# Projections ahead of attention: q with k and p0 with p1 as seven-product pairs in a decoder layer on one Trainium2 core

## The chip, the core and the metric

The kernel runs on one core of a Trainium2 chip. Its engines are TensorE (PE, matrix products, with a queue of its own for loading weights, PEld), VectorE (DVE), ScalarE (ACT) and GpSimd (POOL); SyncE (SP) mostly issues transfers (DMA). Each works through its own queue in order and they meet through semaphores. The metric is the device time of one execution in microseconds (us). A time quoted as the median comes from three executions; a profile shows one execution.

## The reference, cut to what matters

One layer of a hybrid decoder, 512 tokens by 1024 channels, float32. The part that the change touches is the input projection and the attention behind it:

```python
proj = h @ w_in[l]                      # 512x1024 by 1024x4096
q, k, v, p, g = jnp.split(proj, [...])  # 512, 512, 512, 512, 2048 columns
y_attn = moba_attention(q, k, v, rel_bias) @ w_branch_attn[l]     # 8 heads of 64
y_pool = multiscale_pool(p, w_pool_group[l], pool_scale[l]) @ w_branch_pool[l]
gates = sigmoid(g).reshape(B, S, 2, D)
mixed = gates[:, :, 0] * y_attn + gates[:, :, 1] * y_pool
h = layer_norm(ALPHA * h + mixed @ w_out[l], ...)
a, u = split(h @ w_ffn_in[l], 2)        # gated feed-forward with a causal convolution
h = layer_norm(ALPHA * h + (gelu(conv(a)) * u) @ w_ffn_out[l], ...)
```

With 512 tokens the block selection of the attention takes every past block, so it is causal attention with a relative bias. The pooling branch takes, for each of four groups of 128 channels, the mean over the last 2, 4, 8 or 16 tokens minus the token, and multiplies it by a 128x128 matrix.

## The kernel before, in words

**Numbers.** Every float32 operand of a large product is split in a high part (a rounded copy, made by ACT, line 69) and a low part (the difference, made by DVE, line 70), and a product is the sum of three matmuls: high by high, high by low, low by high (`mm3`, lines 211, 214, 215). PE does nothing but such matmuls, the transposes and the small products of attention.

**Tiles.** The projections are computed transposed: a *tile* is 128 output channels by 512 tokens, eight chunks of 128 input channels deep, so 24 matmuls of 512 columns (`in_tile`). Its weights are one *chunk*, 128 by 1024 numbers, loaded by SP into `wraw`, split into `whi` and `wlo`, which are rings of five; chunks are asked for in the order of a list, three ahead of the use (`LEAD`, `weights`, `fetch`). There are four tiles each of q, k and p, and sixteen of g, the gate logits. v is computed first, for all four blocks of tokens at once.

**Seven-product pairs.** Where two tiles are computed together, the product of a 2x2 block matrix is done with seven block products in place of eight (`seven`): products with the chunks A, X, D and Y of the weights, two quarters each for A, X and Y, one for D, each against a quarter of x or a sum of quarters of x. A product is 12 matmuls of 256 columns. A is a plain tile of weights, D is a half of the other one. X is made by a copy (SP) and an accumulating transfer on top of it (POOL, line 163). Y is made of A and X by two sums on DVE (line 173). The sums of quarters of x are called nT1, T3, nT2 and T4 and are formed on DVE (lines 232 and 235, `t_form`) and split. The partial results are copied out by ACT and summed by DVE (lines 252 to 266); the last product of a pair, its closing, is issued behind the first two of the next pair (`flush`). In the kernel before this form is used for eight of the gate tiles (four pairs, `sag`, `sbg`, `scg` in the trace) and for the feed-forward's input (`saf`, `sbf`, `scf`), not for q, k and p.

**The order of the work.** v, q0, k0, p0; then, for each pair of heads, the scores of two heads, two transposes and the product with v, with one tile behind each of the four steps (`bg`, which also issues the pooling product `zb` of a p tile two tiles later). The tiles in this place are the rest of q, k and p and seven g tiles; one g tile remains behind the last product with v. Then come the branch products (`br`), the gate pairs, and the rest of the layer.

**Attention, a head.** `scores`: eight matmuls of high-precision q by k (q in one tile of high and low halves, k in two tiles `k1` and `kl`, made from the tile in `q_done`, `k_done`: lines 382 to 394); DVE adds the bias strip and takes the maximum (line 458); ACT takes the exponentials and sums (line 464); DVE the reciprocal; POOL scales the rows (line 469). `trans`: ten transposes on PE (line 483) and copies out. `pv`: the product with v for two heads (line 496).

**Pooling.** `pool_in`: ACT copies the tile (402), POOL makes the windowed sums by up to four additions (407), DVE makes the difference (410 to 412), which is split. `pool_out` is the small product, `zb`.

Of the kernel before, what the change touches and what calls it, by code (L numbers as in the profile page):

```python
# [19 lines left out]
H = 8  # L20
# [13 lines left out]
TMP = 4  # L34
WARM = 7
NKEEP = 12
# [9 lines left out]
def layer_kernel(ctx: ExitStack, tc: tile.TileContext, xT, x, w_v, w_c, rel_bias, invcnt, w_group,  # L46
# [18 lines left out]
    def split(hi, lo, src, copy=None):  # L65
        if copy:
            copy(hi, src)
        else:
            nc.scalar.activation(hi, src, AF.Copy)  # L69
        nc.vector.tensor_tensor(lo, src, hi.bitcast(F32), op=ALU.subtract)  # L70
# [10 lines left out]
    C0 = len(chunks)  # L81
    chunks += [w_c[first[n] + j] for n, j in order]
# [11 lines left out]

    for f in range(KT - 1):
        add(("br", f), w_br[f])
# [53 lines left out]
    homes = {("g", "A"): araw, ("f", "A"): araw}  # L150
# [133 lines left out]
    keep = keepp.enter_context(tc.tile_pool(name="keep", bufs=1))  # L284
    attn = ExitStack()
    aw = attn.enter_context(tc.tile_pool(name="aw", bufs=2))
# [11 lines left out]
    def load_x(kt, xr, c=slice(0, S), copy=None):  # L298
        state["x"] = nc.sync.dma_start(xr[:, c], xT[kt * P:(kt + 1) * P, c])
        split(xT_hi[:, kt, c], xT_lo[:, kt, c], xr[:, c], copy)  # L300

    for kt in range(KT):
        xr = aw.tile([P, S], F32, tag="tmp", name=f"xr{kt}", bufs=TMP)
        if kt == 0:
            load_x(kt, xr, slice(0, 256), nc.vector.tensor_copy)
            fetch(early=lambda: load_x(kt, xr, slice(256, 512), nc.vector.tensor_copy))
        else:
            load_x(kt, xr)
            if kt % 2 == 0:
                fetch()  # L310
# [15 lines left out]
    wg_raw = aw.tile([P, 4, P], F32, tag="strip", name="wg_raw", bufs=3)  # L326
    nc.sync.dma_start(wg_raw, w_group)
    wg_hi = aw.tile([P, 4, P], F32R, name="wg_hi", bufs=1)
    wg_lo = aw.tile([P, 4, P], F32R, name="wg_lo", bufs=1)
# [4 lines left out]
    F_sb = aw.tile([H, STRIP], F32, tag="pp", name="F_sb", bufs=3)  # L334
# [8 lines left out]
    strips = {}  # L343

    def load_strip(h):
        strips[h] = aw.tile([P, S], F32, tag="strip", name=f"strip{h}", bufs=3)
# [6 lines left out]
    vv = aw.tile([P, NT, H * DH], F32, name="vv", bufs=1)  # L353
# [15 lines left out]
    gates = keep.tile([P, NKEEP, S], F32, name="gates")  # L369
    zT = keep.tile([P, 4, S], F32, name="zT")  # L370
    oT = keep.tile([P, 4, S], F32, name="oT")
# [6 lines left out]
    def q_done(p, b):  # L378
        for e in range(2):
            own, oth = slice(e * DH, (e + 1) * DH), slice((1 - e) * DH, (2 - e) * DH)  # L380
            t = aw.tile([P, S], F32R, tag="q1", name=f"q1_{2 * p + e}", bufs=3)
# [4 lines left out]

    def k_done(p, b):
        for e in range(2):
            own, oth = slice(e * DH, (e + 1) * DH), slice((1 - e) * DH, (2 - e) * DH)
            hi = aw.tile([P, S], F32R, tag="k1", name=f"k1_{2 * p + e}", bufs=3)  # L390
            lo = aw.tile([P, S], F32R, tag="kl", name=f"kl_{2 * p + e}", bufs=3)
            for half in (own, oth):
                nc.scalar.activation(hi[half, :], b[own, :], AF.Copy)
                nc.vector.tensor_tensor(lo[half, :], b[own, :], hi[own, :].bitcast(F32), op=ALU.subtract)
# [3 lines left out]
    def pool_in(j, b):  # L398
        w = POOL_WINDOWS[j]
        pt = aw.tile([P, PAD + S], F32, tag="tmp", name=f"pt{j}", bufs=TMP)  # L400
        nc.gpsimd.memset(pt[:, :PAD], 0.0)
        nc.scalar.activation(pt[:, PAD:], b, AF.Copy)
        cur, sh = pt, 1
        while sh < w:
            nxt = aw.tile([P, PAD + S], F32, tag="tmp", name=f"pw{j}_{sh}", bufs=TMP)
# [3 lines left out]
        d = aw.tile([P, S], F32, tag="tmp", name=f"dif{j}", bufs=TMP)  # L409
# [3 lines left out]
        dh = aw.tile([P, S], F32R, tag="difh", name=f"difh{j}", bufs=2)  # L413
# [611 lines left out]
```

## Time and profile before

| | us |
|---|---|
| median of 3 executions | 645.15 (643.87 to 646.44) |
| the profiled execution | 644.98 |
| its span, first to last instruction | 643.3 |
| PE busy in it | 631.4 (98%) |
| DVE busy | 472.4 (73%) |
| ACT busy | 346.4 (54%) |
| POOL busy | 119.8 (19%) |

The mean granted clock of PE is 0.995 of full speed.

A row of a group reads: line of the kernel, engine, operation, output <- inputs, count, then busy time, mean duration in ns, and the idle time of the engine ahead of these instructions with what ended it. A row of waits: what waited <- what it waited for, then us in total, times, the longest. A row of the timeline: start, duration, engine, line, operation, output <- inputs, count. A row of the table by windows: the window in us, its length, then busy us (and instructions) of PE, PEld, DVE, ACT and POOL, the granted clock of PE, the share of the DMA engines' time, and GB/s. A row of transfers: output <- input, queue, count, size, median us from issue to landing. In the timeline several instructions of a kind stand in one row, with x and their count. A matmul's own duration overlaps the next one's: what a matmul costs in a full stream is the distance of two starts.

### The profile page before, as it was taken

The page shows a single profiled execution, that of the slowest core. Times are in us where ns is not written, and L with a number is a line of the kernel's source. Part 1 is how long each engine was busy: PE and PEld are TensorE (multiplying, and loading weights), DVE is VectorE, ACT ScalarE, POOL GpSimd, SP SyncE. Part 2 cuts the span into 40 slices and gives each one's busy share as a digit, 9 for nine tenths or more (in the row PEclk, how much of TensorE's full clock was granted, in tenths as well). Part 3 has the DMA queues.
Part 4 walks back from the last instruction along what each step waited for, and adds up shares of the span by engine and source line. Part 5 has one row for each costly group of instructions (what it writes and reads, how often), then busy time and mean ns, then how long its engine had stood idle before and what let it go on. Part 6 is the DMA issues. An engine that isn't in the chain of part 4 may idle for free.

```text
span 643.3 us, 9708 instructions
## 1 busy us (share of the span) xinstructions
PE 631.4 (98%) x3730; PEld 555.0 (86%) x3730; DVE 472.4 (73%) x698; ACT 346.4 (54%) x505; POOL 119.8 (19%) x161
## 2 busy tenths in 40 slices
PE   9999999999999999999999999999999999999994
PEld 6888787878788998889999999999998888888884
DVE  6456665564884787499776889888889649788596
ACT  6547556675624557225544566556666346556352
POOL 1505260213052111110010101011002002123202
PEclk9999999999999999999999999999999999999998
DMA  8733222115366415714086576776638956899905
GB/s 303 261 123 103 83 82 83 67 66 186 110 185 158 115 41 191 275 52 165 1 236 171 147 202 160 211 167 198 148 100 297 273 149 131 208 187 206 250 2 130
DMA packets 35294, 100.06 MB, mean 156 GB/s; under 512 B 3880, under 2 KB 4136, under 8 KB 34992
## 3 DMA queue, kind: packets, MB, share of 16 engines
q1 hardware_dynamic: 23920, 67.96, 31.2%
q0 software_dynamic: 10752, 30.43, 23.4%
q10 hardware_dynamic: 576, 1.05, 0.4%
q8 instruction: 29, 0.48, 0.3%
q14 instruction: 17, 0.14, 0.1%
HBM read 96.26 MB, written 3.17 MB: 155 GB/s over the span
## 4 chain that ended last, share of the span: by engine, by line
PE 89%; DMA 4%; DVE 3%; POOL 2%; ACT 1%; issue 1%; SPq 0%; DVEq 0%; ACTq 0%; POOLq 0%
PE fi L214 5%; PE fi L215 5%; PE fi L211 5%; PE saf L211 4%; PE saf L215 4%; PE saf L214 4%; PE v L367 3%; PE g L211 2%; PE g L215 2%; PE g L214 2%; PE br L214 2%; PE br L215 2%; PE wo L214 2%; PE br L211 2%; PE wo L211 2%; PE wo L215 2%
## 5 line engine op out<-in xcount | busy, mean ns | idle before, releaser
L70 DVE TENSOR_TENSOR wlo<-wraw,whi 128x1024 fp32r<-128x1024 f32 (+1 forms) x69 | 84.4, 1228 | 33.3 <-ACT whi L69 32.9
L69 ACT ACTIVATE whi<-wraw 128x1024 fp32r<-128x1024 f32 (+1 forms) x68 | 70.3, 1038 | 59.9 <-PE g L214 8.6
L214 PE MATMUL fi<-hT_lo,whi 128*128 128x512 f32 (+1 forms) x168 | 56.7, 339 | 0.0
L215 PE MATMUL fi<-hT_hi,wlo 128*128 128x512 f32 (+1 forms) x168 | 56.7, 339 | 0.0
L211 PE MATMUL fi<-hT_hi,whi 128*128 128x512 f32 (+1 forms) x168 | 56.4, 340 | 0.0
L70 DVE TENSOR_TENSOR wlo<-araw,whi 128x1024 fp32r<-128x1024 f32 x36 | 43.7, 1221 | 14.5 <-ACT whi L69 13.8
L69 ACT ACTIVATE whi<-araw 128x1024 fp32r<-128x1024 f32 x36 | 37.9, 1060 | 22.1 <-PE br L214 6.4
L163 POOL DMA_DIRECT2D xraw<-in_w_fi x14 | 16.9, 1210 | 162.3 <-DMA xraw<-in_w_fi 85.5
L69 ACT ACTIVATE whi<-tw 128x1024 fp32r<-128x1024 f32 (+1 forms) x30 | 29.3, 983 | 23.6 <-PE fi L214 10.4
L70 DVE TENSOR_TENSOR wlo<-tw,whi 128x1024 fp32r<-128x1024 f32 (+1 forms) x30 | 33.3, 1126 | 7.9 <-ACT whi L69 7.8
L215 PEld LDWEIGHTS fi<-hT_hi,wlo 128*128 128x128 f32 x168 | 31.9, 190 | 3.4
L214 PEld LDWEIGHTS fi<-hT_lo,whi 128*128 128x128 f32 x168 | 31.9, 190 | 3.4
L211 PEld LDWEIGHTS fi<-hT_hi,whi 128*128 128x128 f32 x168 | 31.6, 190 | 3.4
L214 PE MATMUL saf<-hT_lo,whi 128*128 128x256 f32 x112 | 31.6, 282 | 0.0
L211 PE MATMUL saf<-hT_hi,whi 128*128 128x256 f32 x112 | 31.6, 282 | 0.0
L215 PE MATMUL saf<-hT_hi,wlo 128*128 128x256 f32 x112 | 31.5, 282 | 0.0
L211 PE MATMUL sbf<-T_hi,whi 128*128 128x256 f32 x112 | 31.3, 280 | 0.0
L211 PE MATMUL saf<-nT_hi,whi 128*128 128x256 f32 x112 | 31.3, 279 | 0.0
L215 PE MATMUL saf<-nT_hi,wlo 128*128 128x256 f32 x112 | 31.3, 279 | 0.0
L215 PE MATMUL sbf<-T_hi,wlo 128*128 128x256 f32 x112 | 31.2, 279 | 0.0
L214 PE MATMUL saf<-nT_lo,whi 128*128 128x256 f32 x112 | 31.2, 279 | 0.0
L214 PE MATMUL sbf<-T_lo,whi 128*128 128x256 f32 x112 | 31.2, 279 | 0.0
(301 smaller groups left out, 2006.9 us busy)
## 6 DMA issues: line engine op xcount, KB each, us to landing
wraw<-in_w_c SPq DMA_DIRECT2D x20, 512.0 KB, 3.5
tw<-in_w_fo POOLq DMA_DIRECT2D x20, 512.0 KB, 7.0
wraw<-in_w_fi SPq DMA_DIRECT2D x16, 512.0 KB, 3.9
araw<-in_w_fi SPq DMA_DIRECT2D x14, 512.0 KB, 4.5
xraw<-in_w_fi SPq DMA_DIRECT2D x14, 512.0 KB, 4.3
xraw<-in_w_fi POOLq DMA_DIRECT2D x14, 512.0 KB, 6.0
tw<-in_w_fo SPq DMA_DIRECT2D x10, 512.0 KB, 5.0
wraw<-in_w_fo SPq DMA_DIRECT2D x10, 512.0 KB, 9.0
```

The costliest lines, as they stand in the source:

```text
L69: nc.scalar.activation(hi, src, AF.Copy)
L70: nc.vector.tensor_tensor(lo, src, hi.bitcast(F32), op=ALU.subtract)
L163: nc.gpsimd.dma_start(v, bass.AP(tensor=a.tensor, offset=a.offset, ap=[[pst, pn], [u.offset + S - a.offset, 2], [est, S]]), accum_op=ALU.add)
L211: ins = nc.tensor.matmul(out_, wh, ah, start=start, stop=False, **kw)
L214: nc.tensor.matmul(out_, wh, al, start=False, stop=False, **kw)
L215: nc.tensor.matmul(out_, wl, ah, start=False, stop=stop, **kw)
L367: nc.tensor.matmul(bs[j], xs_[j][a], (wh, wl)[b], start=kt == 0 and n == 0, stop=False)
```

## The change

The projections that attention needs are computed ahead of it. After v come p2 and p3 as plain tiles, then five seven-product pairs: p0 with p1, and q with k four times (q0 with k0 and so on). The four sums of x that these need (named `iT...`, `inT...`) are formed in the raw x tiles at the start, and these tiles then serve as homes of the X and D chunks, A chunks go to the ring `wraw`. The second tile of a pair comes out negated, so `k_done` and the copy in `pool_in` get a factor of -1. For each pair ACT or the closing sums leave q and k raw in buffers (`rq`, `rk`); `heads(p)` makes q and k of two heads from them, for the first pair at once, for the others at every second head of the attention.

In attention, scores run two heads ahead of the transposes, and eight g tiles fill the eight steps, one a head, the last of them behind the last transposes. The split of the pooling output zT is done during heads 4 to 7 in program order. The sigmoids of the gate tiles are held back until the last copy of the attention's output. The memory is laid out anew: a pool for the projection phase (`pw`), one for what both phases use (`av`) and one for attention (`aw`). The core of the diff:

```diff
-    order = [("q", 0), ("k", 0), ("p", 0), ("p", 1)]
-    spare = [("p", 2), ("p", 3)] + [("g", 8 * g + f) for f in range(GSEVEN) for g in range(2)]
-    for p in range(1, pairs):
-        order += [("q", p), ("k", p), spare.pop(0), spare.pop(0)]
-    order += spare
...
+    for j in PLAIN:
+        add(("p", j), w_c[first["p"] + j])
+    add_seven(("i", 0), w_c[first["p"]], w_c[first["p"] + 1])
+    for p in range(pairs):
+        add_seven(("i", 1 + p), w_c[first["q"] + p], w_c[first["k"] + p])
+    fill = [("g", 8 * g + f) for f in range(GSEVEN) for g in range(2)]
+    for n, j in fill:
+        add((n, j), w_c[first[n] + j])
...
-    homes = {("g", "A"): araw, ("f", "A"): araw}
+    homes = {(n, "A"): araw for n in "igf"}
...
+    xr = [pw.tile([P, 4, S], F32, name=f"xr{n}") for n in range(2)]
...
+    def heads(p):
+        q_done(p, raw_q[p])
+        k_done(p, raw_k[p])
...
+    with tc.issue_after(state["xlo"].ins):
+        t_form(parts[0], ti, xr[0][:, :, t1], xr[0][:, :, t2], xr[1][:, :, t1], xr[1][:, :, t2])
+    for n in parts[1:]:
+        t_form(n, ti, xr[0][:, :, t1], xr[0][:, :, t2], xr[1][:, :, t1], xr[1][:, :, t2])
+    homes["i", "X"] = lambda n: xr[0][:, n % 2 * 2:n % 2 * 2 + 2, :].rearrange("p a c -> p (a c)")
+    homes["i", "D"] = lambda n: xr[1][:, n % 2, :]
+    for j in PLAIN:
+        in_tile("p", j)
...
+    def pool_done(ba, u):
+        pool_in(0, ba)
+        pool_in(1, u, -1.0)
+
+    def heads_done(p, ba):
+        raw_q[p] = av.tile([P, S], F32, tag="rq", name=f"rq{p}")
+        nc.scalar.activation(raw_q[p], ba, AF.Copy)
+        if p == 0:
+            heads(0)
+
+    for n in range(1 + pairs):
+        if n == 0:
+            u, done = xr[1][:, 3, :], pool_done
+        else:
+            u = raw_k[n - 1] = av.tile([P, S], F32, tag="rk", name=f"rk{n - 1}")
+            done = lambda ba, u, p=n - 1: heads_done(p, ba)
+        seven(("i", n), (xT_hi, xT_lo), ti, xr[1][:, 2, n % 2 * 256:n % 2 * 256 + 256], u, done)
+        if n == 2:
+            for j in PLAIN:
+                pool_out(j)
+        elif n == 4:
+            pool_out(0)
+            pool_out(1)
+    flush()
...
-    bg(3)
-    for p in range(pairs):
-        scores(2 * p)
-        bg()
-        scores(2 * p + 1)
-        bg()
-        trans(2 * p)
-        bg()
-        trans(2 * p + 1)
-        bg()
-        pv(p)
-    bg(len(todo))
+    scores(0)
...
+    scores(1)
+    for h in range(H):
+        if h % 2 == 0 and h + 2 < H:
+            heads(h // 2 + 1)
+        if h < H - 1:
+            in_tile(*fill.pop(0))
+        if h + 2 < H:
+            scores(h + 2)
+        trans(h)
+        if h >= 4:
+            split(zT_hi[:, h - 4, :], zT_lo[:, h - 4, :], zT[:, h - 4, :])
+        if h == H - 1:
+            in_tile(*fill.pop(0))
+        if h % 2:
+            pv(h // 2)
...
-            for g in range(2):
-                nc.scalar.activation(gslot[8 * g + f], gslot[8 * g + f], AF.Sigmoid)
+            with tc.issue_after(state["o"].ins):
+                for g in range(2):
+                    nc.scalar.activation(gslot[8 * g + f], gslot[8 * g + f], AF.Sigmoid)
```

The order in which each engine finally issues its instructions is set by a scheduler from this program order, and is known before the kernel runs; "the built order" below means that.

More of the change, by code (lines that the diff above doesn't have):

```diff
@@ L34 @@
 TMP = 4
+PLAIN = (2, 3)
 WARM = 7
-NKEEP = 12
 KH = NF // 2
@@ L325, in layer_kernel @@
                             compare_op=ALU.is_equal, fill=0.0)
-    wg_raw = aw.tile([P, 4, P], F32, tag="strip", name="wg_raw", bufs=3)
     nc.sync.dma_start(wg_raw, w_group)
-    wg_hi = aw.tile([P, 4, P], F32R, name="wg_hi", bufs=1)
-    wg_lo = aw.tile([P, 4, P], F32R, name="wg_lo", bufs=1)
+    wg_hi, wg_lo = (pw.tile([P, 4, P], F32R, name=f"wg_{q}") for q in ("hi", "lo"))
     split(wg_hi, wg_lo, wg_raw)
@@ L529, in layer_kernel @@
     bp = bra.enter_context(tc.tile_pool(name="bp", bufs=1, reuse_waits="tile"))
-    zT_hi = bp.tile([P, 4, S], F32R, name="zT_hi")
-    zT_lo = bp.tile([P, 4, S], F32R, name="zT_lo")
     oT_hi = bp.tile([P, 4, S], F32R, name="oT_hi")
     oT_lo = bp.tile([P, 4, S], F32R, name="oT_lo")
-    for k in range(4):
-        split(zT_hi[:, k, :], zT_lo[:, k, :], zT[:, k, :])
+    more = bp.tile([P, 4, S], F32, name="more")
     for k in range(4):
@@ L565, in merged @@
         mts[f] = a
-    unused = [gates[:, n, :] for n in range(2 * GSEVEN, NKEEP)]
+    unused = [more[:, n, :] for n in range(4)]
     forms = list(parts)
```

106 lines of the change are left out of this document (50 added, 56 removed).

## The prediction

> **What bounds the kernel now.** I read the busy times first, then what TensorE (PE) waits for, then the table by stretches of time.
>
> ```profile
> PE 631.4 (98%) x3730; PEld 555.0 (86%) x3730; DVE 472.4 (73%) x698; ACT 346.4 (54%) x505; POOL 119.8 (19%) x161
> ```
>
> ```profile
> PE warm_ps L296 <- DVE warm L293: 1.2, 1, 1.2
> PE fod L214 <- DVE wlo L70: 0.6, 1, 0.6
> PE zb L211 <- ACT difh L69: 0.6, 2, 0.3
> PE v L367 <- DVE whi L275: 0.3, 1, 0.3
> ```
>
> ```profile
> 25.00:45.00 20.00, 20.00 (x91) 16.60 (x90) 7.90 (x10) 9.96 (x14) 1.69 (x3) 1.00 0.54 176
> ...
> 345.00:485.00 140.00, 140.00 (x1176) 139.57 (x1175) 118.98 (x165) 83.75 (x124) 14.45 (x12) 1.00 0.65 170
> ```
>
> PE is busy 98% of the span, and the four rows of its waits add up to 2.7 us: matmul time is the time, and any idle time that the change gives PE in the stage it rewrites is added almost whole. In 25 to 45 us (plain projection tiles) VectorE (DVE) works 7.9 of 20 us and could take more. In 345 to 485 us, seven-product pairs of the feed-forward, PE is full but DVE is at 119 of 140 us: this method is paid for by DVE.
>
> **What a pair saves.** In the timeline of PE, q starts at 26.99 and k at 32.43; in the chain of waits the last products of four feed-forward pairs start at:
>
> ```profile
> 26.99 0.39 PE L211 MATMUL q<-xT_hi,whi 128*128 128x512 f32 x1
> 32.43 0.39 PE L211 MATMUL k<-xT_hi,whi 128*128 128x512 f32 x1
> ...
> 50.04 0.28 PE L454 MATMUL sc<-k,q 128*128 128x256 f32 x1
> 51.33 0.40 PE L211 MATMUL q<-xT_hi,whi 128*128 128x512 f32 x1
> ...
> 58.06 0.47 PE L211 MATMUL k<-xT_hi,whi 128*128 128x512 f32 x1
> 58.37 0.39 PE L214 MATMUL k<-xT_lo,whi 128*128 128x512 f32 x1
> ```
>
> ```profile
> 413.79 0.36 PE saf L215 x3
> 473.27 0.36 PE saf L215 x3
> ```
>
> A plain tile of 24 matmuls takes 32.43 - 26.99 = 5.44 us (0.227 each), two take 10.88. Six pairs lie between 413.79 and 473.27: 59.48 / 6 = 9.91 us a pair of 84 matmuls (0.118 each, 1.42 for a product of 12). A pair saves 0.97 us, the five new ones (p0 with p1, four of q with k) **-4.84 us**, as long as PE is fed. The rows also give the eight score matmuls of a head, 51.33 - 50.04 = 1.29 us.
>
> **The order.** More groups of attention now alternate with tiles. 58.06 to 58.37 is 0.31, so a switch costs 0.31 - 0.23 = 0.08 us. The built order has some 12 switches more, because pv is cut by gate tiles: +1.0. The two waits of zb (0.6, above) go, as the pooled inputs are ready long before the pairs at which zb now stands: -0.6. Together **+0.4**.
>
> **Stalls at the first pair.** The chunk X of a pair is a sum of weight quarters: a copy issued by SyncE (SP), an accumulating transfer on top issued by GpSimd (POOL), then the split. Its home is the first half of the raw x, which T3 still uses, so the copy waits until T3 is formed and split on DVE. Rows:
>
> ```profile
> xraw<-in_w_fi SPq DMA_DIRECT2D x14, 512.0 KB, 4.3
> xraw<-in_w_fi POOLq DMA_DIRECT2D x14, 512.0 KB, 6.0
> quad<-in_w_c POOLq DMA_DIRECT2D x4, 512.0 KB, 7.9
> ```
>
> ```profile
> 17.50 0.68 DVE L70 TENSOR_TENSOR xT_lo<-xr,xT_hi 128x512 fp32r<-128x512 f32 x1
> 19.59 0.69 DVE L70 TENSOR_TENSOR wg_lo<-wg_raw,wg_hi 128x512 fp32r<-128x512 f32 x1 [1.41 <-ACT wg_hi L69]
> ...
> 46.61 0.69 DVE L410 SCALAR_TENSOR_TENSOR dif<-pw,pt 128x512 f32<-128x512 f32 x1 [0.23 <-POOL pt L401]
> 47.33 0.29 DVE L458 CUSTOM_DVE_ANT_0 pp<-sc,strip 128x128 f32<-128x128 f32 x1
> 47.55 0.42 DVE L458 CUSTOM_DVE_ANT_0 pp<-sc,strip 128x256 f32<-128x256 f32 x1
> 47.90 0.15 DVE L411 TENSOR_TENSOR dif<-pw,cinv 128x1 f32<-128x1 f32 x1
> 49.05 0.08 DVE L458 DVE_READ_ACCUMULATOR2_ANT nm<- 128x1 f32 x1
> ```
>
> ```profile
> L70 DVE TENSOR_TENSOR wlo<-wraw,whi 128x1024 fp32r<-128x1024 f32 (+1 forms) x69 | 84.4, 1228 | 33.3 <-ACT whi L69 32.9
> ```
>
> ```profile
> L235 DVE SCALAR_TENSOR_TENSOR quad<-quad,quad x2: 1212/1213/1214, 175.4 to 180.5; 128x1024 f32<-128x1024 f32 x2
> ...
> L173 DVE TENSOR_TENSOR araw<-xraw,araw x14: 679/687/694, 339.3 to 470.4; 128x512 f32<-128x512 f32 x14
> ```
>
> (a) The last split of x ends at 17.50 + 0.68 = 18.2. Behind it DVE has, in the built order, three forms (1.21), the low parts of two weight tiles and two forms (1.23) and wg_lo (0.69): 9.2 us, so 27.4. The copy lands 4.3 later, at 31.7; the accumulate 6.0 to 7.9 after that (the two POOL rows), 37.7 to 39.6; two Y sums (0.69) and wlo7 (1.23) follow, 40.3 to 42.2. PE wants it at 4.71 (start of v, as before) + 22.28 (v) + 10.88 (p2, p3) + 2.83 (two products) = 40.7. Between -0.4 and 1.5 I take **+0.9**, nearer the 7.9 row, which is the one that reads this weight tensor. (b) The next splits, wlo9 and wlo10, come 1.76 us apart (1.23, and half of dif2's 0.69 + 2 x 0.15 between them) against a product of 1.42: 2 x 0.33 = **+0.66** (bounds 0 and 1.2). (c) The T4 product waits for a high part that is queued on ScalarE (ACT) behind that of the next X chunk, and so for its accumulate: 0 to 1.2, **+0.6**.
>
> (d) POOL takes its queue in order. The accumulate of the third X chunk stands ahead of p3's four pool additions, and waits for a copy that starts when wlo7 is done (T). Rows:
>
> ```profile
> L407 POOL TENSOR_TENSOR pw<-pt 128x527 f32<-128x527 f32 x4 | 4.7, 1165 | 28.6 <-ACT pt L402 28.5
> ...
> L163 POOL DMA_DIRECT2D xraw<-in_w_fi x14 | 16.9, 1210 | 162.3 <-DMA xraw<-in_w_fi 85.5 <-DVE fT L264 27.4 <-DVE wlo L70 16.8
> ```
>
> T + 4.3 + 1.2 (issue) + 4 x 1.17 = T + 10.2. Then DVE does dif3 (0.69, twice 0.15), two sums (0.42 each), wlo12 (0.68) and the last sum of pair 0 (0.42), all queued at or behind dif3: T + 13.1. PE needs that sum for the closing product of pair 0 after 84 matmuls, T + 9.9 + the 1.3 of (b) and (c) = T + 11.2. **+1.9**, bounds 0 (POOL reaches the additions earlier) and 4.9 (below).
>
> The rest of the pairs: DVE has some 38 us of work in 41.5 us of products between wlo7 and the last pair's chunk (my count of the built order by these durations), ACT 31, so no more stalls there.
>
> **Stalls at the hand-over to attention.** Rows of the timeline for one head, and of the groups:
>
> ```profile
> L394 DVE TENSOR_TENSOR kl<-k,k 64x512 fp32r<-64x512 f32 x16 | 11.0, 687 | 6.8 <-ACT k L393 6.7
> ```
>
> ```profile
> 51.19 0.40 ACT L464 ACTIVATE pp<-pp,nm 128x128 f32<-128x128 f32 x1
> 53.29 0.19 ACT L464 ACTIVATION_READ_ACCUMULATOR pp<-pp,nm 128x1 f32 x1
> ```
>
> ```profile
> 53.80 3.04 POOL L469 TENSOR_SCALAR pp<-pp,rs 128x128 f32<-128x128 f32 x4 [0.51 <-DVE nm L461]
> ...
> 141.45 2.07 POOL L469 TENSOR_SCALAR pp<-pp,rs 128x128 f32<-128x128 f32 x4 [18.35 <-PE g L215]
> ```
>
> Call E the end of head 1's scores. The closing product of the last pair waits for a DVE sum that is queued behind wlo29 and the two kl of head 4. wlo29's high part waits for a ring slot that PE frees only 0.6 before E, and head 4's k waits for E itself. DVE: wlo29 to E + 1.7, kl twice 0.69 to 3.1, the sum 0.42: E + 3.5. PE is idle until then. Then DVE goes on with q1_4 (0.69), the score reductions of heads 0 and 1 (47.33 to 49.13 in the rows above is 1.8 with two dif operations in it, so 1.7 each), three zT_lo (0.69 at 0.64 pitch), the negated maximum (0.2): E + 9.9. Exponentials 51.19 to 53.48, say 2.1 in a row without the load: 12.0. Reciprocal 0.2, and the first three of four scalings on POOL (6 of 10 columns of 2.07 to 3.04: 1.2 to 1.8): E + 13.7. The first transposes need these. PE's own work from E is 1.42 + 5.44 + 1.29 = 8.15. PE loses 13.7 - 8.15 = **+5.5** (3.5 ahead of the closing product, 2.0 ahead of the transposes). Bounds: 3 (wlo29 and the zT_lo slip in elsewhere) and 7. From there PE has 8.9 us a head against DVE 6.9 and ACT 6.6; I find no other stall. The last move is the load of quads, whose place is now used by attention: it starts after the last pv.
>
> ```profile
> 163.57 0.50 PE L211 MATMUL g<-xT_hi,whi 128*128 128x512 f32 x1
> ...
> 207.22 0.28 PE L211 MATMUL sag<-xT_hi,whi 128*128 128x256 f32 x1
> ```
>
> In the kernel before, the last pv ends at 163.57 and the gate pairs that use quads start at 207.22; without the tile between, 38.2 us remain, and load, four forms, copy and accumulate are needed within them: some 28 us by the durations above and my count of DVE's order (the load taken as an accumulate's 6.0 to 7.9). Cost nothing; if DVE's branch work delays the forms by over 10 us, the excess is added.
>
> **Sum.** -4.84 + 0.4 + 0.9 + 0.66 + 0.6 + 1.9 + 5.5 = +5.1. Against the profiled execution, 644.98 us, that is 650.1; the median of the runs, 645.15, lies 0.17 above it, so 650.3. A change of 0.5% is 3.2 us, about what a measurement of this kernel tells from no change.
>
> [...]
>
> ```profile
> 635.00:640.00 5.00, 0.00 (x0) 0.00 (x0) 3.85 (x10) 0.80 (x2) 0.72 (x1) 0.71 0.78 208
> 640.00:643.30 3.30, 0.00 (x0) 0.00 (x0) 0.00 (x0) 0.00 (x0) 0.00 (x0) 0.50 0.32 122
> ```
>
> PE's last matmul ends near 634, and the granted clock is 0.71 over the next 5 us and 0.50 after: it falls to half some 3 us into idleness. So the gap may cost a stretch at half clock; what it costs is hidden as long as PE waits 2.0 us for the transposes anyway, so I add nothing. [...]
>
> **Rivals.** (1) Faster: the stalls are hidden, because the scheduler's order leaves DVE more room than my hand chain gives: the five pairs keep their 4.84 less 0.4, and 645.15 - 4.4 = 640.7. For it: DVE is idle 12 of 20 us in 25 to 45. Against it: the sum for E + 3.5 is in DVE's order behind work that is released by E. It decides if all stalls together stay under 1.2 us (4.4 less the 3.2 of 0.5%). (2) No change: the pair phase runs without stalls, and only the hand-over costs: -4.84 + 0.4 + 5.5 gives 646.2. For it: (a) to (d) rest on landing times that may be 2 us shorter. (3) Slower than forecast: the additions and accumulates on POOL slow down beside DVE. One row has it:
>
> ```profile
> 83.88 1.92 POOL L407 TENSOR_TENSOR pw<-pw 128x525 f32<-128x525 f32 x1
> ```
>
> At 1.92 for each of p3's four additions (d) grows by 4 x 0.75 = 3.0, the three of p0 and p1 by 2.3, and each accumulate at 7.9 in a pair phase where DVE is 92% full turns its delay into PE's: 655 to 658. [...]
>
> **How the numbers follow.** Forecast 0.45 (648.4 to 653.5), rival 1 0.12, rival 2 0.25 (643 to 648), rival 3 0.18. The range 643.5 to 657 leaves out rival 1 and the top of rival 3, about 0.18. Faster 0.12, same 0.25, slower 0.63.
>
> **What would show it.** PE's waits in the profile after: a row for the first X product of pair 0 near 41 us, one for its closing product on a DVE sum, one of about 3.5 for the last pair's closing product, one of about 2 for tr on POOL's scaling. Pairs free of waits should start 9.9 us apart. If q and k pairs run at 9.9 and tr doesn't wait, rival 1 holds. Wrong I would be above all if DVE's pitch is shorter than its busy time, or if accumulates land in 4 us.

## The result, and the profile after

The changed kernel takes 661.29 us (median, 660.70 to 662.12), the kernel before 644.65 (643.87 to 646.44) in the same comparison: a ratio of 1.0255 (1.0229 to 1.0281). It is slower by 16.6 us, where +5.1 was forecast, and lies above the forecast range. The profiled execution of the changed kernel took 662.12, its span is 660.4 and its mean granted clock 0.987. From here *before* and *after* are the two kernels.

The busy times of after, and what PE waits for:

```profile
PE 638.0 (97%) x3910; PEld 566.3 (86%) x3910; DVE 497.9 (75%) x741; ACT 355.0 (54%) x530; POOL 133.0 (20%) x166
```

```profile
PE sai L212 <- DVE sai L266: 6.1, 2, 4.1
PE sbi L212 <- ACT whi L69: 3.7, 1, 3.7
PE sai L216 <- DVE wlo L70: 1.3, 1, 1.3
PE warm_ps L306 <- DVE warm L303: 1.2, 1, 1.2
PE sbi L216 <- DVE wlo L70: 0.9, 1, 0.9
```

Waits of 2.7 us have become 13.2. The waits for zb are gone, as forecast. PE's busy time has also risen, by 6.6 us, although five pairs should need 4.84 us less: waits alone don't tell the story.

Where the time went is told by the first branch product, which both kernels reach after the same work. In the timelines of before and of after:

```profile
169.14 0.39 PE L211 MATMUL br<-zT_hi,whi 128*128 128x512 f32 x1
```

```profile
187.24 0.50 PE L212 MATMUL br<-zT_hi,whi 128*128 128x512 f32 x1
```

After is 18.1 us late there, and wins 1.0 behind it (span 17.1 longer). So everything happened in the stage that was rewritten, and what follows is unhurt. In this stage, PE has three long gaps. They are shown here (timeline of after; the bracket is the idle time ahead of the instruction), and below them the table by windows for the time behind each gap:

```profile
44.13 0.39 PE L212 MATMUL sbi<-iT_hi,whi 128*128 128x256 f32 x1 [3.73 <-ACT whi L69]
...
59.34 0.58 PE L212 MATMUL sai<-xT_hi,whi 128*128 128x256 f32 x1 [2.03 <-DVE sai L266]
...
107.86 0.58 PE L212 MATMUL sai<-xT_hi,whi 128*128 128x256 f32 x1 [4.06 <-DVE sai L266]
```

```profile
45.90:49.10 3.20, 3.20 (x17) 3.20 (x17) 3.20 (x6) 2.29 (x4) 0.00 (x0) 0.50 0.67 208
59.30:62.30 3.00, 2.96 (x14) 2.96 (x15) 2.97 (x4) 1.69 (x4) 0.13 (x2) 0.50 0.90 186
63.00:91.00 28.00, 26.65 (x216) 25.87 (x215) 26.03 (x39) 20.81 (x35) 5.29 (x5) 1.00 0.40 108
107.50:113.50 6.00, 5.64 (x19) 5.04 (x20) 5.99 (x21) 3.58 (x5) 1.18 (x2) 0.50 0.39 125
```

The first is the first X product of pair 0, the second its closing product, the third the closing product of the last pair. After each, the granted clock (third number from the end) is 0.50 for 3 to 6 us. What half clock does to a matmul is seen in two pairs of neighbours:

```profile
111.01 0.63 PE L215 MATMUL g<-xT_lo,whi 128*128 128x512 f32 x1
111.44 0.63 PE L216 MATMUL g<-xT_hi,wlo 128*128 128x512 f32 x1
...
114.21 0.40 PE L212 MATMUL g<-xT_hi,whi 128*128 128x512 f32 x1
114.44 0.40 PE L215 MATMUL g<-xT_lo,whi 128*128 128x512 f32 x1
```

A pitch of 0.43 us in place of 0.23, so 47% of such a stretch is lost: 1.5 + 1.4 + 2.8 = 5.7 us in the three. In the row of 63 to 91 us, DVE works 26.0 of 28.0 us: the pairs leave it little room.

The last part is the product with v. One of before and its counterparts in after (timeline; x counts the matmuls that ran without another in between):

```profile
71.90 2.37 PE L496 MATMUL ob<-PT,vv 128*64 128x512 f32 x16
```

```profile
128.02 1.07 PE L543 MATMUL ob<-PT,vv 128*64 128x512 f32 x2
129.02 0.51 PE L212 MATMUL g<-xT_hi,whi 128*128 128x512 f32 x1
...
133.60 1.07 PE L543 MATMUL ob<-PT,vv 128*64 128x512 f32 x4
...
136.19 1.51 PE L543 MATMUL ob<-PT,vv 128*64 128x384 f32 x10
137.63 0.39 PE L501 MATMUL sc<-k,q 128*128 128x256 f32 x1
```

Sixteen matmuls in one go take 2.3 us from start to start of the next (71.90 to 74.21). Cut into 2, 4 and 10 they take 1.00 + 1.00 + 1.44 = 3.44. Each is 128*64 in the rows, where the projections are 128*128, and the two heads write different halves of the output. In before the sixteen start in pairs, the first at 71.90 and 71.91 us, the second at 72.38 and 72.39: two heads' matmuls run beside each other. Where the scheduler draws them apart, they no longer do: in the first piece of after the two matmuls of 512 columns, of one head alone, start at 128.02 and 128.50. They take 1.00 us, and at that price the sixteen, which have 320 columns on average, would take some 5 us (an estimate) and not 2.3. Three of the four products with v are cut like this.

### The profile page after: what moved, and what is told of

Read it like the earlier page. It is cut to its first block, busy times and chain, and to the rows that moved or that the text cites. A ratio compares the mean times of both kernels' runs of the same rounds, so it can differ in the third digit from the quotient of the medians.

```text
span 660.4 us, 10178 instructions
## 1 busy us (share of the span) xinstructions
PE 638.0 (97%) x3910; PEld 566.3 (86%) x3910; DVE 497.9 (75%) x741; ACT 355.0 (54%) x530; POOL 133.0 (20%) x166
## 4 chain that ended last, share of the span: by engine, by line
PE 86%; DVE 4%; POOL 4%; DMA 3%; issue 2%; ACT 1%; SPq 0%; DVEq 0%; POOLq 0%
PE fi L212 4%; PE fi L216 4%; PE fi L215 4%; PE saf L212 4%; PE saf L216 4%; PE saf L215 4%; POOL F_sb L347 3%; PE g L212 2%; PE g L216 2%; PE g L215 2%; PE br L212 2%; PE wo L216 2%; PE br L216 2%; PE br L215 2%; PE wo L215 2%; PE wo L212 2%
## 5 line engine op out<-in xcount | busy, mean ns | idle before, releaser
L70 DVE TENSOR_TENSOR wlo<-wraw,whi 128x1024 fp32r<-128x1024 f32 (+1 forms) x59 | 72.2, 1231 | 18.7 <-ACT whi L69 18.6
L69 ACT ACTIVATE whi<-wraw 128x1024 fp32r<-128x1024 f32 (+1 forms) x58 | 59.6, 1034 | 45.6 <-DMA wraw<-in_w_fo 9.0
L70 DVE TENSOR_TENSOR wlo<-araw,whi 128x1024 fp32r<-128x1024 f32 x46 | 57.8, 1263 | 10.1 <-ACT whi L69 9.4
L69 ACT ACTIVATE whi<-araw 128x1024 fp32r<-128x1024 f32 x46 | 48.2, 1058 | 19.7 <-PE saf L215 6.1
L212 PE MATMUL saf<-hT_hi,whi 128*128 128x256 f32 x112 | 31.7, 283 | 0.0
```

The source lines that it names most:

```text
L70: return nc.vector.tensor_tensor(lo, src, hi.bitcast(F32), op=ALU.subtract)
L212: ins = nc.tensor.matmul(out_, wh, ah, start=start, stop=False, **kw)
```

## The experiments

Unless it says otherwise, each kernel computes the same as after. Ratios are to before on the same chip; where after is compared, its 1.0255 is meant, and by the intervals a difference of two ratios is uncertain by some 2 us.

**The first gap: POOL's queue.** The X chunk's accumulate is in POOL's queue, and what stood ahead of it is in the timeline of after:

```profile
14.46 17.46 POOL L347 COPY F_sb<-rel 8x1 f32<-8x1 f32 x32 [12.91 <-DMA rel<-in_rel_bias]
32.23 0.76 POOL L349 DMA_DIRECT2D F_d<-F_sb  x1 [0.32 <-POOL F_sb L347]
34.78 1.69 POOL L353 DMA_DIRECT2D strip<-F_d  x3 [1.79 <-DMA F_d<-F_sb]
36.45 2.55 POOL L164 DMA_DIRECT2D xr<-in_w_c  x2
```

The construction of the bias strip, 32 tiny copies, waits for `rel` until 14.46, takes 17.46 us, and only then the accumulate may go, at 36.45. The first experiment brings `rel` in early, on POOL's own queue ahead of x.

```diff
+    rel = const.tile([H, N_BUCKETS], F32, name="rel")
+    nc.gpsimd.dma_start(rel, rel_bias)
     def load_x(kt, xk, c=slice(0, S), copy=None):
...
-    rel = const.tile([H, N_BUCKETS], F32, name="rel")
-    nc.sync.dma_start(rel, rel_bias)
```

> Edit: only the load of the 8x32 bias table is moved: GpSimd's queue issues it first, instead of SP after x. In the changed kernel (661.29 us) the 32 small copies into F_sb take GpSimd 17.5 us (14.5 to 31.9) and the accumulate of pair 0's X chunk is issued behind them and the strips, at 36.45. Theory 1 (GpSimd's queue holds the accumulate back, and PE's gap of 3.7 + 0.9 us at 40 to 46 us comes from it): the copies end near 20 to 25, the accumulate is issued near 29, the gap falls under 0.5 us, and with it the stretch at half clock behind it: 5 to 7 us less, 654 to 656. Theory 2 (the landing of X itself, or DVE's queue of splits, sets it): gap as before, 661 +- 1.

663.11 us, ratio 1.0302 (1.0281 to 1.0323): no gain, and by the ratios 0.5% more than after, of which the two profiled executions (662.26 and 662.12) show nothing. The accumulate in POOL's timeline, and PE's longest waits, in this kernel:

```profile
31.86 2.52 POOL L164 DMA_DIRECT2D xr<-in_w_c  x2 [7.60 <-DMA xr<-in_w_c]
```

```profile
PE tr L531 <- POOL pp L517: 6.6, 1, 6.6
PE sai L212 <- ACT whi L69: 3.1, 1, 3.1
PE sai L212 <- DVE sai L266: 2.1, 1, 2.1
```

POOL is now idle for 7.60 us and issues the accumulate when SP's copy lands, at 31.86. The row for sbi is gone: the cause of the first gap is POOL's queue, not the landing time. The gain isn't kept. The last closing product starts at 101.74 (107.86 in after), 6.1 us earlier, but the first exponentials start at 113.24, against 113.72 in after: the negated maximum waits on DVE behind four splits of zT and one of a weight tile until 110.4, and ACT then has the k and q of the next two heads (111.94 - 110.00 = 1.9 us) ahead of them. PE waits 6.6 us for the first transposes, and half clock follows that wait (0.50 from 116.8 to 120.0). The first branch product comes at 187.33, where it was.

**Are the half-clock stretches a cost of their own?** Matmuls whose result nobody uses were put into the gaps of the first and last pairs (26 and 14, and 28).

```diff
+        for _ in range(idle[0]):
+            tc.keep_in_program_order(nc.tensor.matmul(bb[:, 256:], warm[:, :P], warm[:, :256], start=True, stop=True))
         s_mm(key, "X", 0, tt["T3"], low, True, idle[0])
```

> Edit: PE is given matmuls without use (bf16, 256 columns, into a half bank that is not read) in front of the three matmuls that wait longest: 26 ahead of pair 0's first X product, 14 ahead of its closing, 28 ahead of the last pair's closing. They fill some 2.8, 1.5 and 3.0 us of idle time, no wait is removed. Theory 1 (a gap of 2 us and more costs its own length and then 3 to 6 us at half clock): granted clock 1.00 throughout, waits end when they did, 3.3 to 6.3 us less (the stretches at half clock last 3.3, 3.0 and 6.0 us, half of each is lost; the last may be hidden by the first transposes' wait): 655 to 658. Theory 2 (the half clock in the records costs nothing in time, or DVE sets the pace anyway): 661 +- 1.

666.06 us, 1.0347 (1.0326 to 1.0368).

```profile
PE sbi L273 <- DVE xr L264: 4.3, 1, 4.3
PE tr L535 <- POOL pp L521: 1.7, 1, 1.7
```

As a total it is inconclusive: the filling matmuls of pair 0 write a PSUM bank that DVE reads, and so wait themselves (first row). At the hand-over it tells something: with the gap filled the clock stays at 1.00, the closing product takes 1.44 us (2.73 in after) and the first gate tile 5.47 (7.05). The 2.9 us are the price of the half clock there. They are not kept: PE then waits 1.7 us for POOL's scaling (second row), the very wait that the forecast had said would hide them, and runs at half clock behind it (0.50 from 120.3 to 123.7). From the start of the closing product to the fourth head's scores this kernel takes 18.7 us, after 17.7.

**The cut product with v.** It is issued one gate tile later, its matmuls kept together.

```diff
-                nc.tensor.matmul(b[e * DH:(e + 1) * DH, kb * P:], vv[:, kb, h * DH:(h + 1) * DH],
-                                 PTs[h][:, toff[kb]:toff[kb] + n], start=kb == 0, stop=kb == NT - 1)
+                tc.keep_in_program_order(
+                    nc.tensor.matmul(b[e * DH:(e + 1) * DH, kb * P:], vv[:, kb, h * DH:(h + 1) * DH],
+                                     PTs[h][:, toff[kb]:toff[kb] + n], start=kb == 0, stop=kb == NT - 1))
...
+        if h % 2 == 0 and h:
+            pv(h // 2 - 1)
         if h + 2 < H:
             scores(h + 2)
...
-        if h % 2:
-            pv(h // 2)
+    pv(H // 2 - 1)
```

> Edit: the product with v of a pair of heads is issued as one block behind the next gate tile, its matmuls for the two heads next to each other. In the changed kernel three of four of these products are cut in three pieces by gate tiles and take 1.00 + 1.00 + 1.44 = 3.44 us against 2.30 whole. Theory 1 (the matmuls of the two heads use different halves of the columns and run beside each other only when they are neighbours): 2.30 each again, 3 x 1.14 = 3.4 us less, and the gate tiles (5.55 to 6.04 us against 5.44) lose about 1 more: 656.5 to 658. Theory 2 (each piece costs only a switch of 0.08 us): at most 1 us less, 660 to 661.

656.18 us, 1.0192 (1.0175 to 1.0209), 0.63% below after: 4.1 us by the ratios, 5.1 by the medians.

```profile
131.82 2.38 PE L546 MATMUL ob<-PT,vv 128*64 128x512 f32 x16
```

The products are whole and take 2.4 us again. Three of them give back 3 x 1.14 = 3.4. From the first transposes to the first branch product it takes 63.3 us in place of 68.3; the rest of these 5.0 us falls to the tiles that are no longer interrupted.

**Is the hand-over cured by work in between?** The closing product of the last pair is put behind the first gate tile.

```diff
-    flush()
...
             in_tile(*fill.pop(0))
+        if h == 0:
+            with tc.issue_after(state["mm"].ins):
+                flush()
```

> Edit: the closing product of the last pair is issued behind the first gate tile instead of ahead of it, so that PE has 5.44 us of work while DVE gets to the sum that the closing waits for. Theory 1 (that wait alone costs the time: 4.06 us of gap and the half clock behind it): about 7 us less, 654. Theory 2 (DVE's queue from the end of head 1's scores to the first transposes is one chain, and it ends when it ends): the gap of 4.06 goes, and a wait of tr for GpSimd's scaling of 4 to 6 us appears in its place; what is won is only the half clock, 0 to 3 us: 658 to 661.

660.32 us, 1.0255 (1.0235 to 1.0274): no different from after.

```profile
PE g L212 <- DVE sai L266: 4.1, 1, 4.1
```

The same 4.1 us, in front of the gate tile. The kernel has eight banks of PSUM in rotation (its pool `ps`), so the gate tile's bank is, in all likelihood, one that this very DVE sum has to free. An independent piece of work isn't independent when it needs the buffer. So this did not test the idea, but points at the sum's place in DVE's queue.

**That place.** The preparation of the next heads (and the splits of zT) are held back on DVE and ACT until the scores' maximum and exponentials are issued (`behind_soft`).

```diff
         if h % 2 == 0 and h + 2 < H:
-            heads(h // 2 + 1)
+            with behind_soft(h - 1):
+                heads(h // 2 + 1)
```

> Edit: in attention, the preparation of the next heads (q1, k1, kl) and the split of zT are held on DVE and ACT behind the softmax of the head that PE needs next; nothing else changes. In the changed kernel DVE did wlo, kl twice, q1, the two heads' reductions and four zT_lo between the end of head 1's scores (103.4) and the exponentials of head 0 (113.7), and the first transposes came at 118.9. Theory 1 (this queue on DVE sets when PE goes on; the gap of 4.06 and the half clock lie inside it): the closing's wait falls to about 2.5, the transposes come 4 to 6 us earlier, 655 to 658. Theory 2 (PE's own gap and clock set it, the softmax is early enough): only kl's 1.4 us are won, 659 to 661.

658.55 us, 1.0225 (1.0206 to 1.0245), 1.9 us below after by the ratios, which is no more than their uncertainty; in the traces the first transposes come 3.3 us earlier (115.65 and 118.93), less than the first theory's 4 to 6, and the wait at the hand-over goes from 4.1 to 2.8. The two `kl` (1.38 us) no longer stand ahead of the sum on DVE; the split of the weight tile (1.22) still does.

**Are the pairs the cause?** Ten plain tiles in place of five pairs, the rest as in after.

```diff
-        seven(("i", n), (xT_hi, xT_lo), ti, xr[1][:, 2, n % 2 * 256:n % 2 * 256 + 256], u, done)
+        for key in (("p", 0), ("p", 1)) if n == 0 else (("q", n - 1), ("k", n - 1)):
+            in_tile(*key)
```

> Edit: the new order is kept, but the five pairs are computed as ten plain tiles (24 matmuls of 512 columns each) in place of seven products; the four forms of x for them and the X, D and Y chunks go with them. Theory 1 (the pairs' stalls, 6.7 at the first X product, 3.8 at the first closing, 1.4 in the middle, cost more than the 4.84 us that their matmuls save): 661.3 + 4.8 - 11.9 = 654, with 650 to 657 as the stall at the hand-over may shrink too, because the last closing is gone. Theory 2 (the new order itself costs the time and the pairs are a gain): 664 to 666. On GpSimd the 32 small copies into F_sb should take near 8 us again as before the change, not 17.5, if it is DVE's work on the forms beside them that stretches them.

655.12 us, 1.0165 (1.0142 to 1.0188), 6 us below after. PE waits for nothing in the ten tiles; it waits 4.7 us for POOL ahead of the transposes. A second part of the loss, 10.6 us to before by the ratios, thus remains without the pairs.

**The cures together.** Early `rel`, whole products with v, and `behind_soft`; once with the pairs, once with plain tiles.

> Edit: three edits at once: the bias table loaded first by GpSimd, the product with v whole, and the next heads' preparation held behind the softmax. Theory 1 (three separate causes: first X product 6, cut products with v 5.1, queue ahead of the softmax 5): 661.3 - 16 = 645, from 643 to 648. Theory 2 (DVE's total work from the first pair to the first transposes sets the time, so that what is won at the first pair is lost again at the hand-over, as when the table alone was moved): 650 to 653.

> Edit: the same three edits, and the five pairs as ten plain tiles. What is left of the pairs' saving when the other causes are gone: if pairs without stalls are worth their 4.84 us, this is 3 to 5 us slower than with pairs; if their remaining stalls (first closing, splits in the middle) take it back, it is within 1 us of it or faster. Time 645 to 650 by theory 1.

With pairs 649.57 us, 1.0088 (1.0070 to 1.0107). With plain tiles 644.67, 1.0020 (1.0007 to 1.0032). The first branch product of the two:

```profile
174.95 0.50 PE L212 MATMUL br<-zT_hi,whi 128*128 128x512 f32 x1
```

```profile
169.95 0.50 PE L214 MATMUL br<-zT_hi,whi 128*128 128x512 f32 x1
```

The three cures take away 10.8 of the 16.4 us by the ratios (11.7 by the medians), less than the 16 that the first theory expected; the time lies just under the second's 650 to 653. With plain tiles the kernel is nearly as fast as before (+1.3 us by the ratios), so most of what was left in the run above was the attention's. The pairs, meant to save 4.84, cost 4.9 (4.4 by the ratios). What PE waits for in the kernel with pairs:

```profile
PE sai L212 <- ACT whi L69: 3.1, 1, 3.1
PE sai L212 <- DVE sai L266: 2.1, 1, 2.1
PE sai L212 <- ACT xr L253: 1.3, 1, 1.3
...
PE sai L216 <- DVE wlo L70: 1.1, 1, 1.1
```

These are 7.6 us of waits, and stretches at half clock stand behind two of them. In the longest, DVE itself had been idle:

```profile
51.96 0.69 DVE L420 SCALAR_TENSOR_TENSOR dif<-pw,pt 128x512 f32<-128x512 f32 x1 [2.32 <-POOL pw L417]
```

It waits 2.3 us for POOL's additions of p3, and ACT and PE wait behind it: a chain of queues, not a full DVE.

**p3's difference later.** The difference of p3 stands ahead of pair 0's sums on DVE (step (d)). It is put behind the last sum, once in after alone, once in the kernel with the cures.

```diff
+        def rest():
             d = pw.tile([P, S], F32, tag="tmp", name=f"dif{j}", bufs=TMP)
...
+        if j == 3:
+            late.append(rest)
...
+            with tc.issue_after(state["sum"].ins):
+                late.pop(0)()
```

> Edit: the three edits of the run with all three (649.57), and the difference of p3 (pooled minus token) is taken on DVE behind pair 0's last sum instead of ahead of it. In that run PE waited 3.1 us at 52 to 55 for a high part that stood behind this difference on ACT and DVE, whose input comes from GpSimd's four additions, which stand behind an accumulate; half clock followed until 58.6. Theory 1 (that queueing costs its wait and the half clock): 3.1 + 1.7 less, 644 to 646. Theory 2 (DVE's total work in the pairs is the limit and the wait moves to the next product): 648 to 650.

> Edit: of the changed kernel (661.29), only p3's difference on DVE moved behind pair 0's last sum. It prices the fourth stall of the prediction, put at 1.9 us, alone: by its trace 2.0 us of waiting at the closing of pair 0 and 1.6 at half clock, so 657 to 659 if they are won in full; 660 to 661.5 if the hand-over takes it back, as it did when the bias table alone was moved.

In after alone: 657.70 us, 1.0219 (1.0204 to 1.0234). The wait for pair 0's closing product is gone, for 2.3 us by the ratios (3.6 by the medians), which fits the 2.0 of the gap and part or all of the half clock behind it. With the cures: 651.62, 1.0122 (1.0105 to 1.0139), by 2.2 us slower than without the edit. In the profiled executions nearly all of the difference (2.8 of 3.1 us) lies ahead of the first tile of p, which the edit doesn't touch; from there to the first branch product they take 148.7 us with the edit and 148.5 without it. So nothing is gained. The 3.1 us that the kernel with the cures waits at 55 us are gone; three new waits (0.6, 1.0, 0.4) stand at 78 to 81 us, half clock follows them, and the wait at the hand-over is 2.6 in place of 2.1. From 60 to 90 us:

```profile
60.00:90.00 30.00, 28.02 (x212) 27.05 (x211) 27.90 (x41) 20.85 (x35) 5.83 (x5) 0.94 0.42 105
```

DVE is at 27.9 of 30 us (at 3.97 of 4 from 75 to 79, just where two of the new waits begin) and the clock at 0.94: the work that was moved met the next pairs there. To that kernel one more edit was added, the first gate tile and behind it the closing product, both between the scores of heads 0 and 1:

```diff
-    flush()
...
+    in_tile(*fill.pop(0))
+    with tc.issue_after(state["mm"].ins):
+        flush()
     scores(1)
```

> Edit: the same, and the first gate tile and then the closing of the last pair are put between the scores of head 0 and head 1, so that fewer than eight PSUM banks are asked for and PE has 5.4 us of work while DVE gets to the sum that the closing needs. In the run with all three edits PE waited 2.1 us there and ran at half clock behind it (a gate tile of 6.85 in place of 5.44 us). Theory 1 (that gap is the last of the hand-over's cost): 3 to 4 us less than the run with p3's difference moved, 640 to 642, which is 2 to 4 us under the kernel before (643.7). Theory 2 (the softmax of head 0 ends no sooner, and the first transposes wait instead): less than 1 us.

650.98 us, 1.0112 (1.0094 to 1.0130), 0.6 us less, as the second theory had it. The wait at the hand-over for the sum is gone (1.2 and 1.2 us remain ahead of transposes), and the same stretch reads

```profile
60.00:90.00 30.00, 27.70 (x205) 26.45 (x204) 28.52 (x42) 21.09 (x35) 4.34 (x4) 0.94 0.34 89
```

with DVE at 28.5 of 30. So whatever is cured at one place, PE is held up at another. That DVE has nothing to spare is the likeliest reason here, but it was only read from these windows.

**Fewer pairs.** If DVE is the limit, two pairs (q0 with k0, q2 with k2) with plain tiles between should run without waits.

```diff
+PAIRED = (0, 2)
...
+        elif p in PAIRED:
             u = raw_k[p] = av.tile([P, S], F32, tag="rk", name=f"rk{p}")
...
+        else:
+            in_tile("q", p)
+            flush()
+            in_tile("k", p)
```

> Edit: the three edits of before (table first, product with v whole, next heads' preparation held), and of the five pairs only q0 with k0 and q2 with k2 are seven-product pairs; p0, p1, q1, k1, q3, k3 are plain tiles and stand between them. Theory 1 (back to back, a pair asks DVE for more than the 9.9 us it takes PE, and every stall is DVE, ACT and GpSimd being late; with plain tiles between them DVE has the time): no waits in the pair phase, and 2 x 0.97 us less than with ten plain tiles (which stood 0.2% over the kernel before): 0.1% to 0.3% under the kernel before, 641 to 643 where that has 643.3. Theory 2 (a pair's stalls come with it wherever it stands, from its chunk X and from the queues): 645 to 648.

PE's waits (its first row, 1.2 us for the warming-up matmuls, is that of all kernels), the table by windows and the first branch product:

```profile
PE sai L218 <- ACT xr L259: 0.4, 1, 0.4
PE v L380 <- DVE whi L282: 0.3, 1, 0.3
```

```profile
42.00:102.00 60.00, 59.60 (x348) 52.67 (x347) 41.10 (x70) 35.60 (x58) 11.77 (x11) 1.00 0.33 105
```

```profile
167.56 0.50 PE L218 MATMUL br<-zT_hi,whi 128*128 128x512 f32 x1
```

PE is all but full (one wait of 0.4 us), DVE at 41 of 60 us, and the first branch product comes 2.4 us earlier than with plain tiles only, against 1.94 that two pairs should save, and 1.6 earlier than in before. The whole kernel takes 644.27, 1.0020 (1.0007 to 1.0033), where the first theory had 641 to 643: it doesn't beat before, and it has the same ratio as ten plain tiles (1.0020). The profiled execution, the one that these rows are from, took 642.70 and is the shortest of twelve, and the rows of before are from an execution of 644.98, where the median of before in this comparison is 643.33. So the 1.6 us are not a shown gain, and that two pairs save 2 us is seen in this one execution only. Why not in the median is open. The plain tiles also give ACT, GpSimd and the transfers more time, so this run doesn't separate DVE from them. No version tried here is faster than before.

## Why the prediction was right or wrong

The experiments are called e1 to e12 here, in the order e1 (early `rel`), e2 (filled gaps), e3 (whole products with v), e4 (gate tile first), e5 (`behind_soft`), e6 (plain tiles), e7 and e8 (the cures with pairs, and with plain tiles), e9 (with p3's difference late), e10 (and the closing product between the scores), e11 (p3's difference late in after alone), e12 (two pairs).

The direction and the places were right, the size was not: +5.1 forecast, +16.6 found. To the 18.1 us at the first branch product, step by step:

| step | forecast | after |
|---|---|---|
| saving of five pairs | -4.84 | -4.84 (taken over; 2.4 for two pairs in e12's one trace) |
| order: switches and zb | +0.4 | -0.6 for zb, +4 to 5 for cut products with v |
| (a) to (c), first pair | +2.2 | 3.7 + 0.9 of waits |
| (d), closing of pair 0 | +1.9 | 2.0 |
| rest of the pairs | 0 | 1.3 |
| hand-over | +5.5 | 4.1 |
| half clock | 0 | 5.7 (1.5 in the first pair, 1.4 behind (d), 2.8 at the hand-over) |

The last column adds to some 17, within 2 us of 18.1; the half-clock figures are worked out from pitches and the cut product from e3, so it can't be closer. Against the forecast the terms are over by 3 to 4 us (order), 2.9 (half clock in pair 0), 2.4 (first pair's waits), 1.4 (hand-over, its half clock included) and 1.3 (rest of the pairs): no single step explains the miss.

**(a) failed at POOL's queue.** The copy's landing at 31.7 came out in e1, where POOL sends the accumulate at 31.86, released by that copy, but by luck: T3's split was done at 24.9 in after (25.3 in e1) and not at 27.4, and the release came 6.6 us after the copy's issue at 25.28, not 4.3. What the step left out is that POOL takes its queue in order, and the bias strip was in it. In before the same 32 copies are harmless:

```profile
15.16 7.83 POOL L340 COPY F_sb<-rel 8x1 f32<-8x1 f32 x32 [1.86 <-DMA rel<-in_rel_bias]
```

They are done at 23 there. In after they start 0.7 us earlier and take 9.6 us more; with F_d and the strip behind them that takes POOL to 36.45, 4.6 us past the 31.86 of e1. The step had been warned: (d) uses the very rule, that POOL takes its queue in order, four steps further on.

**The order term failed at what a switch costs.** 0.08 us a switch was taken from a score to a tile. A cut product with v costs another thing, the overlap of two heads' matmuls: 1.14 us each. That the products were cut was known; that whole ones overlap stood in before's rows (16 matmuls of up to 512 columns in 2.3 us) and was not read.

**The half clock was put at nothing.** The argument was that PE would wait for the transposes anyway. At the hand-over this held for the larger part. With E at 103.80, where PE goes idle, the three scalings that the first transposes need end at about 117.9 (POOL's four take 2.08 us from 116.33), so at E + 14.1 where E + 13.7 was forecast; PE is there at 118.93, straight behind the scores. So the slow tile had used up the wait and took some 1.0 us more, and e2, which avoids it there, wins nothing. The argument didn't reach the two stretches in pair 0, behind the X product and behind (d): 1.5 + 1.4 = 2.9 us with no later wait beside them. The forecast had read some 3 us of idleness off the end of before and applied it to its gap of 3.5 us; the gaps of 3.73 and 4.06 us are longer than that, but the gap of 2.03 us at pair 0's closing is followed by 3.0 us at 0.50 as well, while one of 2.08 us in e1 is followed by matmuls 0.12 us apart, at full clock. So a gap of 2 us isn't safe either; what decides was not shown (last section).

**(d) was right** in mechanism and size. The timeline of POOL in after has the accumulate ahead of p3's additions, and these at 5.4 us for four, 0.7 over the forecast:

```profile
50.48 1.20 POOL L164 DMA_DIRECT2D xr<-in_w_c  x1 [7.93 <-ACT difs L69]
51.25 1.52 POOL L416 TENSOR_TENSOR pw<-pt 128x527 f32<-128x527 f32 x1
52.85 3.89 POOL L416 TENSOR_TENSOR pw<-pw 128x525 f32<-128x525 f32 x3
```

PE waits 2.03 for the closing product (forecast 1.9), and e11 takes it away by the work named.

**The hand-over was right in mechanism.** 3.5 us ahead of the closing product were forecast and 4.06 came, for the sum queued behind the weight tile and the two kl, as the timeline of DVE shows:

```profile
104.96 1.22 DVE L70 TENSOR_TENSOR wlo<-wraw,whi 128x1024 fp32r<-128x1024 f32 x1
106.09 1.38 DVE L398 SCALAR_TENSOR_TENSOR kl<-rk,k 64x512 fp32r<-64x512 f32 x2
107.39 0.41 DVE L266 TENSOR_TENSOR sai<-xr,sci 128x256 f32<-128x256 f32 x1
```

The 2.0 us forecast for the transposes were used up by the half clock.

**"No more stalls there" failed by 1.3 us.** 38 of 41.5 us of DVE was a fair count (26.0 of 28 in 63 to 91). That little room is the likeliest reason why the cures of e9 and e10 only move the waits on, and why five pairs in a row cost 4.9 us in e7 against e8. It isn't shown as the one cause: e7's longest wait is a chain through POOL with DVE idle for 2.3 us of it.

**The rivals.** The first two, no stalls or only the hand-over, fell. The third named the right neighbourhood, POOL beside DVE, at the wrong instructions: p3's additions grew by 0.7 and not 3.0, the bias copies by 9.6. It gave 655 to 658, nearest of all, in part by luck.

## What to carry to other kernels

Before a transfer is priced by its landing, list everything that stands ahead of its issue in that queue, work of another kind included, and let its time grow if its neighbour gets busier (the bias copies took 7.83 us with DVE busy 59% beside them, 17.46 with 86%). The three gaps of PE in after, of 2.03 to 4.06 us, cost their length and then an estimated 1.4 to 2.8 us more in half-clock matmuls; one of 2.08 us in e1 cost its length alone. Put the larger price in the sum for every such gap, and set it off only against a wait that stands right behind that gap. A method that trades matmul time for VectorE time needs room on VectorE and on the queues that feed it: five pairs in a row, meant to save 4.84 us, cost 4.9, and two among plain tiles ran almost without waits in the one execution that was traced, though the median shows no gain.

## What the runs showed of the hardware

The 32 copies of 8 rows on POOL took 7.83 us in before, 9.34 in e6, 14.11 in e7 and 17.46 in after. The copies are the same; what differs most between the windows of before and of after is DVE's share:

```profile
15.20:23.00 7.80, 7.80 (x36) 6.47 (x35) 4.58 (x6) 6.08 (x8) 7.79 (x32) 1.00 0.70 241
```

```profile
14.50:31.90 17.40, 17.40 (x78) 14.43 (x77) 15.02 (x14) 11.79 (x15) 17.40 (x32) 1.00 0.68 222
```

DVE is busy 59% of the first and 86% of the second stretch (third pair of numbers), there with forms and splits; in e6, which leaves out the forms, it is busy 67%, in e7 87%. The trace of after shows it copy by copy: those that start at 19.20, 20.34 and 21.47 take 1.19 us each, beside DVE instructions that start at 19.14, 20.27 and 21.41 and take 1.22. DVE is done with this work at 29.54, and then thirteen copies together take less than two of these:

```profile
29.89 2.02 POOL L347 COPY F_sb<-rel 8x3 f32<-8x3 f32 x13
```

So beside this DVE stream a copy, 0.18 us at its shortest, took 1.19 us, about as long as the DVE instruction beside it, and from 18.07 to 28.28 only one went by per instruction. What makes the copies longer was not tested by itself: no run changed DVE's work there and nothing else.

The half clock behind a gap differs from gap to gap. In after the granted clock is 0.50 from 45.66, 59.31 and 107.10 us on, for 3.41, 3.41 and 6.83 us; the gaps are those of 3.73 (with one of 0.93 behind it), 2.03 and 4.06 us. The length of a gap alone doesn't tell what follows. Behind the 2.08 us of e7, which end at 101.65, matmuls of 512 columns start 0.43 us apart from 103.39 on, and the clock of 102 to 106 us is 0.61. Behind the 2.08 us of e1, which end at 101.74, matmuls of 256 columns start 0.12 us apart, and the clock of 100 to 110 us is 1.00. And in e3, where PE waits 4.1 us at the hand-over as in after, the clock of 100 to 125 us is 0.93, where after has 0.86: by these means some 3.5 us at half clock in place of 7 (an estimate). What decides was not shown, so the price of a gap was known here only once it was measured.
